# A hybrid decoder layer on one core: weights loaded and split eight blocks at a time instead of four

## The chip, the cores and the metric

The kernel runs on one core of one Trainium2 chip. The metric is the device time of one execution in microseconds (us); the execution is also described by a profile, whose page and trace are quoted here. TensorE (PE) multiplies, VectorE (DVE), ScalarE (ACT) and GpSimd (POOL) do the rest, and SyncE (SP) issues every DMA of this kernel in one queue.

## What is computed

One layer of a decoder on 2048 prompt tokens and 8 one-token samples, 1024 channels wide, all in float32:

```python
h = rmsnorm(x)                                   # norm_pre_mix
q, k, v, z, b, a, mq, mk, mv, mo, mi, mf = split(h @ w_in)          # 3584 columns and 16 gate columns
o_gdn = rmsnorm(gated_delta_rule(conv_silu(q, k, v), ...)) * silu(z)  # 4 heads, chunkwise
h_ml  = sigmoid(mo) * rmsnorm(mlstm(mq, mk, mv, mi, mf))              # 4 heads, chunkwise
x = x + rmsnorm(concat(o_gdn, h_ml) @ w_out)
x = x + rmsnorm(relu(rmsnorm(x) @ w_up) ** 2 @ w_down)               # 4096 hidden channels
```

The outputs are the tokens, the final states of the prompt and the updated states of the samples.

## The kernel before

The prompt is cut into four segments of 512 tokens; the samples ride along with segment 1 (520 columns, worked in two pieces of 260). For each segment the kernel runs the input projection (`a_units`, weights `w_a` and `w_gate`), the two mixers, the output projection (`b_units`, weights `w_o`, worked twice over 256 tokens), and the MLP (`cd_units`, weights `w_up` and `w_dn`). Segments overlap: the mixers and norms of one segment are generators ("streams") that are stepped between the large products of another.

Every large product works on blocks of 128x128 weights. Weights and activations are split into a high and a low float32r part, and a product is three matmuls: high weights by high and by low activations (lines 195 and 196), low weights by high activations (line 200). A **half** (class `Half`) is four weight blocks side by side, a tile of 128x512: `load` brings it into a raw tile `wraw` (four of these, 256 KB), `split` makes its two parts in a tile `whl` (three of these): ACT casts the high part (line 178) and DVE subtracts it from the raw tile for the low part (line 183). `go` issues the 12 matmuls of a half for each piece of columns. A **unit** is two halves; in the projections and the up products both add into one bank of PSUM (`bk`, three banks), in the down products each half has a bank of its own. A raw tile is free for the next load when its split is done, a `whl` tile when the last matmul that reads it is done.

`play` walks the list `main` and sets how far ahead loads and splits are written: at a half it writes the split of the next one and the loads of the four after that, the split with a raised priority (`tc.high_priority(300)`). A scheduler then orders each engine's instructions; every engine, SP's queue included, runs its list in order, so that an instruction that waits holds up what stands behind it. In segment 3 the last states of the samples are worked (`sample_states`): their loads (`st_S`, `st_C`, `dvs`) and stores (`o_sS`, `o_sC`, `o_sn`) share SP's queue with the weights. The products of the last eighth of the MLP run once for each half of the tokens; in segment 3 their split weights are kept for the second half (`keep`, `same`).

Of the kernel before, what the change touches and what calls it, by code (L numbers as in the profile page):

```python
# [24 lines left out]
def program(tc, ctx, d, T):  # L25
# [32 lines left out]
    def r4(t, a=4):  # L58
        return t[:, :].rearrange("p (a b) -> p a b", a=a)

# [25 lines left out]
    w0 = []  # L86
    gain = const([128, 4, 8], "gain")  # channel-major: before and after the mixing, before and after the MLP
    for tt, tag in enumerate(("xt", "xt", "qk", "qk")):
        if tt == 2:
            Q.dma_start(gain, d["gains"])  # L90
            for i in range(2):
                w0.append(sb([128, 512], "wraw", 4))
                Q.dma_start(w0[i], d["w_gate"][:, i * 512:(i + 1) * 512])
        t = sb([128, 1040], tag, 2)
        Q.dma_start(t[:, :1024], d["x_prompt"][tt * 128:(tt + 1) * 128])
        x0.append(t)
        xs0.append(big[:, tt * 1024:(tt + 1) * 1024] if tt < 2 else sb([128, 1040], "xs", 3)[:, :1024])
# [23 lines left out]
    P1 = const([128, 4, 32], "P1")  # L121
# [35 lines left out]
    class Half:  # L157
        """four weight blocks against four activation blocks, each product in three passes; packed weights come twice,
        in columns 32 k + 0..3 and 32 k + 4..7, for the high and the low part of them side by side"""

        def __init__(self, src, acts, parts, first, last, done=None, packed=False):
            self.src, self.acts, self.parts, self.first, self.last, self.done = src, acts, parts, first, last, done
            self.packed = packed
            self.raw = self.hl = self.same = self.keep = None
            self.bank = bk

        def load(self):
            if self.same is not None or self.raw is not None:
                return
            self.raw = sb([128, 512], "wraw", 4)  # L170
            Q.dma_start(self.raw, self.src)

        def split(self):
            if self.same is not None:
                self.hl = self.same.hl
                return
            self.hl = sb([128, 2, 512], "whl", 3, F32R) if self.keep is None else self.keep()
            A.copy(self.hl[:, 0], self.raw)  # L178
            raw, hi, lo = self.raw[:, :], self.hl[:, 0], self.hl[:, 1]
            if self.packed:  # L180
                raw, hi = (t.rearrange("p (a b) -> p a b", b=32)[:, :, 4:8] for t in (raw, hi))
                lo = hi
            V.tensor_tensor(lo, raw, hi.bitcast(F32), op=ALU.subtract)  # L183

        def go(self, part=None):
            acts = self.acts()
            sel = range(len(self.parts)) if part is None else [part]
            for i in sel:
# [4 lines left out]
                for k in range(4):  # L193
                    w = self.hl[:, 0, k * 128:(k + 1) * 128]
# [3 lines left out]
                for k in range(0 if self.packed else 4):  # L198
                    w = self.hl[:, 1, k * 128:(k + 1) * 128]
# [7 lines left out]
    def unit(src, acts, cols, done, packed=False):  # L207
        """acts: a function for the two halves of the activations"""
        parts = [(None, c0, c1) for c0, c1 in cols]
        return [Half(src[:, i * 512:(i + 1) * 512], lambda i=i: acts()[i], parts, i == 0, i == 1, done, packed)  # L210
                for i in range(2)]
# [14 lines left out]
    def norm_a(xt, n, xs=None):  # L226
        """rows / rms"""
        if xs is None:
            xs = sb([128, 1040], "xs", 3)[:, :1024]
# [6 lines left out]
    def norm_b(rows, n, col, gain, halves, bank):  # L236
        """the rows of some token tiles, n tokens in all, to channel-major, times the gain, in two parts"""
# [96 lines left out]
    def a_units(s, halves, order=range(28)):  # L334
# [25 lines left out]
        if s == 0:  # L360
            # the first three of them by token halves, while the second half is being normalised
# [6 lines left out]
    def log1p_exp(L, ab, shape_n):  # L368
        """L = log1p(exp(-ab)), ab >= 0."""
# [1204 lines left out]
```

## Time and profile before

| what | value |
|---|---|
| median of three runs | 2701.5 us (2699.88 to 2704.51) |
| profiled execution, span from first to last instruction | 2703.2 us |
| busy time of PE, DVE, ACT, POOL | 2605.9, 1730.3, 1284.0, 412.8 us |
| mean granted clock of TensorE | 0.989 |
| DMA traffic | 377.41 MB, mean 140 GB/s |

The profiled execution has no time of its own beside its span; the span lies 1.7 us above the median, inside the range of the runs. A busy share is that of the whole span and says nothing about a single stage. In a timeline row the figures are start and duration in us, and the bracket tells how long the engine had been idle before the instruction and what ended that.

### The profile page before, as it was taken

What the parts mean: (1) busy time and instruction counts of PE and PEld (TensorE: products, weight loads), DVE (VectorE), ACT (ScalarE), POOL (GpSimd) and SP (SyncE); (2) the same over time, 40 slices, a digit from 0 to 9 for tenths busy, and PEclk for the clock granted to TensorE, in tenths of its full rate; (3) what the DMA queues carried; (4) which work ended last, traced back from release to release, by engine and by line L of the source; (5) the groups of instructions that cost most, each with busy time, mean ns of one, the idle gap of its engine ahead of it and who ended that gap; (6) DMA issues with size and microseconds to landing.
All of it is one profiled execution on the core that took longest, in us unless ns stands there. A gap on an engine that the chain in (4) does not pass through costs nothing.

```text
span 2703.2 us, 44345 instructions
## 1 busy us (share of the span) xinstructions
PE 2605.9 (96%) x15907; PEld 2271.5 (84%) x15907; DVE 1730.3 (64%) x3508; ACT 1284.0 (48%) x3119; POOL 412.8 (15%) x470
## 2 busy tenths in 40 slices
PE   8999999999999999999799999999999999978998
PEld 6889999778888788878699999997787888766887
DVE  6765768647757557765575865587667567754445
ACT  5636457435535345644455354465363455422332
POOL 2101012311000002420000000062000004430002
PEclk9999999999999999999899999999999999999999
DMA  4444457553323245744433243454242346664222
GB/s 167 156 150 141 145 165 224 193 160 133 102 92 122 99 152 171 238 165 141 97 99 117 95 152 111 153 180 144 88 129 98 123 146 205 205 149 105 94 96 84
DMA packets 319261, 377.41 MB, mean 140 GB/s; under 512 B 53289, under 2 KB 177129, under 8 KB 319033
## 3 DMA queue, kind: packets, MB, share of 16 engines
q1 hardware_dynamic: 319040, 374.57, 44.0%
q8 instruction: 126, 2.06, 0.3%
q14 instruction: 95, 0.77, 0.1%
HBM read 314.04 MB, written 60.53 MB: 139 GB/s over the span
## 4 chain that ended last, share of the span: by engine, by line
PE 83%; DMA 6%; DVE 5%; issue 2%; ACT 2%; POOL 1%; SPq 1%; DVEq 0%; ACTq 0%; POOLq 0%
PE bk L195 25%; PE bk L196 25%; PE bk L200 24%; DVE whl L183 2%; DMA wraw<-w_o 1%; DMA xt<-x_prompt 1%; DVE nt L1197 1%; DMA wraw<-w_up 1%; DVE X L1201 1%; PE mx L563 1%; ACT whl L178 1%; DMA xt<-dO 1%; DMA dqkv<-tB 1%; PE mx L655 1%; PE mx L770 1%
## 5 line engine op out<-in xcount | busy, mean ns | idle before, releaser
L178 ACT CAST whl<-wraw 128x512 fp32r<-128x512 f32 x872 | 539.2, 620 | 972.6 <-PE bk L200 828.6
L183 DVE TENSOR_TENSOR whl<-wraw,whl 128x512 fp32r<-128x512 f32 (+1 forms) x872 | 646.5, 744 | 490.3 <-ACT whl L178 476.1
L195 PE MATMUL bk<-Y,whl 128*128 128x512 f32 (+2 forms) x2208 | 733.2, 346 | 5.7 <-ACT whl L178 3.8
L196 PE MATMUL bk<-Y,whl 128*128 128x512 f32 (+2 forms) x2208 | 731.4, 345 | 0.0
L195 PE MATMUL bk<-X,whl 128*128 128x512 f32 (+3 forms) x2024 | 659.1, 342 | 46.4 <-ACT whl L178 31.8
L196 PE MATMUL bk<-X,whl 128*128 128x512 f32 (+3 forms) x2024 | 656.6, 341 | 2.7 <-DVE X L1201 2.5
L200 PE MATMUL bk<-Y,whl 128*128 128x512 f32 (+2 forms) x2176 | 488.3, 344 | 8.8 <-DVE whl L183 8.8
L195 PEld LDWEIGHTS bk<-Y,whl 128*128 128x128 f32 x2208 | 415.8, 188 | 60.8 <-ACT whl L178 5.9
L195 PEld LDWEIGHTS bk<-X,whl 128*128 128x128 f32 x2024 | 384.1, 190 | 91.7 <-ACT whl L178 35.3
L196 PEld LDWEIGHTS bk<-Y,whl 128*128 128x128 f32 x2208 | 416.7, 189 | 50.3
L200 PE MATMUL bk<-X,whl 128*128 128x512 f32 (+3 forms) x2024 | 442.5, 339 | 8.3 <-DVE whl L183 8.2
L196 PEld LDWEIGHTS bk<-X,whl 128*128 128x128 f32 x2024 | 384.3, 190 | 47.6 <-DVE X L1201 4.1
L200 PEld LDWEIGHTS bk<-Y,whl 128*128 128x128 f32 x2176 | 358.9, 189 | 62.1 <-DVE whl L183 11.5
L200 PEld LDWEIGHTS bk<-X,whl 128*128 128x128 f32 x2024 | 326.6, 189 | 54.1 <-DVE whl L183 11.4
L1245 DVE TENSOR_TENSOR acc<-acc,bk 128x512 f32<-128x512 f32 (+2 forms) x296 | 164.1, 556 | 151.8 <-PE bk L200 147.7
L1124 POOL TENSOR_TENSOR NQ<-NQ,nt 128x256 f32<-128x256 f32 (+4 forms) x145 | 142.8, 988 | 499.0 <-ACT nt L1123 492.1
L1234 DVE TENSOR_TENSOR tB<-tB 128x512 f32<-128x512 f32 (+1 forms) x160 | 93.8, 588 | 55.7 <-ACT Y L1233 54.7
L305 DVE SCALAR_TENSOR_TENSOR tB<-tA,cw,tB 128x512 f32<-128x512 f32 x144 | 107.9, 750 | 13.7 <-ACT tB L301 11.0
L1235 DVE TENSOR_TENSOR Y<-tB,Y 128x512 fp32r<-128x512 f32 (+1 forms) x160 | 97.6, 612 | 3.2
L1232 ACT ACTIVATE tB<-bk 128x512 f32<-128x512 f32 (+1 forms) x160 | 81.7, 511 | 29.2 <-DMA dqkv<-tB 13.1
L1233 ACT ACTIVATE Y<-tB 128x512 fp32r<-128x512 f32 (+1 forms) x160 | 87.3, 549 | 4.3
L596 DVE TENSOR_TENSOR W<-xt 32x30 f32<-32x30 f32 (+14 forms) x240 | 76.2, 317 | 20.0 <-DMA xt<-dn 15.2
(380 smaller groups left out, 2456.4 us busy)
## 6 DMA issues: line engine op xcount, KB each, us to landing
wraw<-w_dn SPq DMA_DIRECT2D x264, 256.0 KB, 2.6
wraw<-w_up SPq DMA_DIRECT2D x256, 256.0 KB, 2.6
wraw<-w_a SPq DMA_DIRECT2D x224, 256.0 KB, 2.8
wraw<-w_o SPq DMA_DIRECT2D x128, 256.0 KB, 3.5
dqkv<-tB SPq DMA_DIRECT2D x48, 256.0 KB, 2.8
gb<-drb SPq DMA_DIRECT2D x32, 256.0 KB, 3.9
qk<-dqkv SPq DMA_DIRECT2D x16, 512.0 KB, 3.7
dzo<-tB SPq DMA_DIRECT2D x32, 256.0 KB, 3.2
```

What stands on the lines that cost most here:

```text
L178: A.copy(self.hl[:, 0], self.raw)
L183: V.tensor_tensor(lo, raw, hi.bitcast(F32), op=ALU.subtract)
L195: PE.matmul(o, lhsT=w, rhs=acts[:, k, 0, c0:c1], start=(self.first and k == 0), stop=False)
L196: PE.matmul(o, lhsT=w, rhs=acts[:, k, 1, c0:c1], start=False, stop=(self.packed and self.last and k == 3))
L200: PE.matmul(o, lhsT=w, rhs=acts[:, k, 0, c0:c1], start=False, stop=(self.last and k == 3))
L305: V.scalar_tensor_tensor(acc, pre[:, t:t + SEG], cw[:, j, t:t + 1], acc, op0=ALU.mult, op1=ALU.add)
L1124: G.tensor_tensor(total[:, c0:c1], total[:, c0:c1], sq[:, c0:c1], op=ALU.add)
L1232: A.activation(r[:, :n], p[:, :n], AF.Relu)
L1233: A.activation(sl[:, 0, c0:c1], r[:, :n], AF.Square)
L1234: V.tensor_tensor(r[:, :n], r[:, :n], r[:, :n], op=ALU.mult)
L1235: V.tensor_tensor(sl[:, 1, c0:c1], r[:, :n], sl[:, 0, c0:c1].bitcast(F32), op=ALU.subtract)
L1245: V.tensor_tensor(a, a, p[:, :c1 - c0], op=ALU.add)
```

## The change

A new class `Weights` holds eight blocks: one raw tile of 128x1024 (two of these instead of four of 128x512), one DMA of 512 KB instead of two of 256 KB, one tile `whl` for both parts (two of 128x2x1024 instead of three of 128x2x512), one cast and one subtraction of 128x1024 instead of two of 128x512. A `Half` now names a `Weights` object and a side of it; in the down products two neighbouring output blocks share one. `play` counts in `Weights`: it writes the split of the next one at the second side of the present one, and keeps two loads written ahead of the last split. The gate weights at the start come in one DMA. In segment 3 the kept weights of the last eighth are two tiles for each `Weights`, so these are still cast and subtracted in pieces of 128x512. To make room, the constant `elast` becomes a broadcast column of `ident`, the scratch tile `P1` of the 32x32 inverses becomes a part of `P2`, and some tiles shrink from 1040 to 1024 columns.

```diff
-    elast = const([128, 128], "elast")
-    G.affine_select(elast, ones, pattern=[[0, 128]], compare_op=ALU.is_ge, fill=0.0, base=-127,
-                    channel_multiplier=1)
-
-    pairsum = const([128, 16], "pairsum")  # high and low part of each gate, added
+    elast = ident[:, 127:128].broadcast_to([128, 128])
...
+    w0 = sb([128, 1024], "wraw", 2)
...
-            for i in range(2):
-                w0.append(sb([128, 512], "wraw", 4))
-                Q.dma_start(w0[i], d["w_gate"][:, i * 512:(i + 1) * 512])
+            Q.dma_start(w0, d["w_gate"])
...
-    P1 = const([128, 4, 32], "P1")
...
+    class Weights:
+        def __init__(self, src, packed=False):
+            self.src, self.packed = src, packed
+            self.raw = self.hl = self.keep = None
+            self.done = False
+        def load(self):
+            if self.raw is None:
+                self.raw = sb([128, 1024], "wraw", 2)
+                Q.dma_start(self.raw, self.src)
+        def split(self):
+            self.hl = sb([128, 2, 1024], "whl", 2, F32R) if self.keep is None else self.keep()
+            for hi, lo, raw in self.pieces():
+                A.copy(hi, raw)
+            for hi, lo, raw in self.pieces():
+                raw, hi = raw, hi
+                if self.packed:
+                    raw, hi = (t.rearrange("p (a b) -> p a b", b=32)[:, :, 4:8] for t in (raw, hi))
+                    lo = hi
+                V.tensor_tensor(lo, raw, hi.bitcast(F32), op=ALU.subtract)
+        def pieces(self):
+            if isinstance(self.hl, list):
+                return [(t[:, 0], t[:, 1], self.raw[:, i * 512:(i + 1) * 512]) for i, t in enumerate(self.hl)]
+            return [(self.hl[:, 0], self.hl[:, 1], self.raw[:, :])]
+        def half(self, i):
+            if isinstance(self.hl, list):
+                return self.hl[i][:, 0], self.hl[i][:, 1]
+            return (self.hl[:, k, i * 512:(i + 1) * 512] for k in range(2))
...
+        def __init__(self, w, side, acts, parts, first, last, done=None):
+            self.w, self.side, self.acts, self.parts = w, side, acts, parts
+            self.first, self.last, self.done, self.packed = first, last, done, w.packed
             self.bank = bk
-
-        def load(self):
-            if self.same is not None or self.raw is not None:
-                return
-            self.raw = sb([128, 512], "wraw", 4)
-            Q.dma_start(self.raw, self.src)
-
-        def split(self):
-            if self.same is not None:
-                self.hl = self.same.hl
-                return
-            self.hl = sb([128, 2, 512], "whl", 3, F32R) if self.keep is None else self.keep()
-            A.copy(self.hl[:, 0], self.raw)
-            raw, hi, lo = self.raw[:, :], self.hl[:, 0], self.hl[:, 1]
-            if self.packed:
-                raw, hi = (t.rearrange("p (a b) -> p a b", b=32)[:, :, 4:8] for t in (raw, hi))
-                lo = hi
-            V.tensor_tensor(lo, raw, hi.bitcast(F32), op=ALU.subtract)
 
         def go(self, part=None):
             acts = self.acts()
+            whi, wlo = self.w.half(self.side)
...
-                    w = self.hl[:, 0, k * 128:(k + 1) * 128]
+                    w = whi[:, k * 128:(k + 1) * 128]
...
-                    w = self.hl[:, 1, k * 128:(k + 1) * 128]
+                    w = wlo[:, k * 128:(k + 1) * 128]
...
+        w = Weights(src, packed)
+        return [Half(w, i, lambda i=i: acts()[i], parts, i == 0, i == 1, done) for i in range(2)]
...
-                A.copy(P1[r:r + 32], pv[r:r + 32])
+                A.copy(P2[r:r + 32, :, 0:32], pv[r:r + 32])
...
-            src = d["w_dn"][e, j // 2][:, (j % 2) * 512:(j % 2 + 1) * 512]
-            return [Half(src, lambda: uT[e], [(None, c0, c1) for c0, c1 in cols], True, True, evac)]
+            if j % 2 == 0:
+                pair[:] = [Weights(d["w_dn"][e, j // 2])]
+            return [Half(pair[0], j % 2, lambda: uT[e], [(None, c0, c1) for c0, c1 in cols], True, True, evac)]
...
-        halves = []
+        ws = []
         for it in main:
             h = it[0] if isinstance(it, tuple) else it
-            if isinstance(h, Half) and h not in halves[-4:]:
-                halves.append(h)
-        place = {id(h): i for i, h in enumerate(halves)}
+            if isinstance(h, Half) and not any(h.w is w for w in ws[-3:]) and not h.w.done:
+                h.w.done = True
+                ws.append(h.w)
+        place = {id(w): i for i, w in enumerate(ws)}
         loaded = split = 0
         for it in main:
             h, part = it if isinstance(it, tuple) else (it, None)
             if not isinstance(h, Half):
                 it()
                 continue
-            n = place[id(h)]
-            while split < min(n + 2, len(halves)):
-                while loaded < min(split + 4, len(halves)):
-                    halves[loaded].load()
+            n = place[id(h.w)]
+            while split < min(n + 2, len(ws)) and (split <= n or h.side == 1 or ws[split].keep is not None):
+                while loaded < min(split + 2, len(ws)):
+                    ws[loaded].load()
                     loaded += 1
                 with tc.high_priority(300):
-                    halves[split].split()
+                    ws[split].split()
                 split += 1
-            while loaded < min(split + 4, len(halves)):
-                halves[loaded].load()
+            while loaded < min(split + 2, len(ws)):
+                ws[loaded].load()
...
+        return [kept[-1][:, i, :, :512] for i in (j % 4, j % 4 + 1)]
...
-        h0.keep, h1.same = lambda j=j: place(j), h0
+        if j % 2 == 0:
+            h0.w.keep = lambda j=j: place(j)
+        h1.w = h0.w
```

The lists of three engines show what moves. First ScalarE at the entry to the output projection of segment 2; line 1084 casts the last tile of its input, line 1093 copies a finished bank, lines 1120 and 1123 square it. Before:

```order
L178 CAST whl<-wraw 128x512
L1084 CAST X_18782<-xt 128x2x256
L178 CAST whl<-wraw 128x512 x7
L1093 COPY Y_19079<-bk 128x256
L1120 ACTIVATE NQ<-bk 128x256
L178 CAST whl<-wraw 128x512 x2
L1093 COPY Y_19079<-bk 128x256
L1123 ACTIVATE nt<-bk 128x256
```

The same place with the change, where the weights' cast is line 169 and the others are 1096, 1105, 1132 and 1135:

```order
L169 CAST whl<-wraw 128x1024
L1096 CAST X_17415<-xt 128x2x256 x2
L169 CAST whl<-wraw 128x1024 x3
L1105 COPY Y_17692<-bk 128x256
L1132 ACTIVATE NQ<-bk 128x256
L169 CAST whl<-wraw 128x1024
L1105 COPY Y_17692<-bk 128x256
L1135 ACTIVATE nt<-bk 128x256
```

For each unit one cast stands where two stood, ahead of the same two readers of the bank; at the entry three of them, for six halves, stand where seven halves stood.

Second SyncE's queue in segment 3, from the stores of the second pair of sample states (`o_sC`, `o_sn`) on. Before:

```order
L171 DMA wraw<-w_up 128x512 x3
L1039 DMA o_sC<-xt 64x8x128
L1040 DMA o_sn<-xt 64x8x1
L171 DMA wraw<-w_up 128x512
L1039 DMA o_sC<-xt 64x8x128
L1040 DMA o_sn<-xt 64x8x1
L171 DMA wraw<-w_up 128x512
L171 DMA wraw<-w_dn 128x512 x8
```

With the change:

```order
L164 DMA wraw<-w_up 128x1024 x2
L1051 DMA o_sC<-xt 64x8x128
L1052 DMA o_sn<-xt 64x8x1
L1051 DMA o_sC<-xt 64x8x128
L1052 DMA o_sn<-xt 64x8x1
L164 DMA wraw<-w_up 128x1024
L164 DMA wraw<-w_dn 128x1024 x4
```

Before, one half of `w_up` is issued between the two pairs of stores and one behind them; with the change one load of 128x1024 stands behind both pairs. Up to the first of these stores both lists issue the same number of weight blocks.

Third ScalarE at the start, around the square of the first tile of segment 1 (line 231, then 243) for which a load of `x_prompt` must land. Before:

```order
L178 CAST whl<-wraw 128x512
L231 ACTIVATE xs,st<-xt 128x1024
L178 CAST whl<-wraw 128x512 x2
L338 ACTIVATE grow<-mx,gbias 128x256
L300 COPY tA<-bk 128x256
L301 ACTIVATE tB<-bk,cw 128x256
L178 CAST whl<-wraw 128x512
```

With the change:

```order
L350 ACTIVATE grow<-mx,gbias 128x256
L243 ACTIVATE xs,st<-xt 128x1024
L312 COPY tA<-bk 128x256
L313 ACTIVATE tB<-bk,cw 128x256
L169 CAST whl<-wraw 128x1024
L350 ACTIVATE grow<-mx,gbias 128x256
L169 CAST whl<-wraw 128x1024
```

The square still stands ahead of the cast of the second unit's weights; two readers of a bank (lines 312 and 313) now stand between them, and the cast is one of 128x1024.

## Rows read from the trace of the kernel before

**Rows 1.** The page: span, then busy time, share and instructions of each engine.

```profile
span 2703.2 us, 44345 instructions
PE 2605.9 (96%) x15907; PEld 2271.5 (84%) x15907; DVE 1730.3 (64%) x3508; ACT 1284.0 (48%) x3119; POOL 412.8 (15%) x470
```

**Rows 2.** The page: groups, busy us, mean ns, then idle before and releasers.

```profile
L178 ACT CAST whl<-wraw 128x512 fp32r<-128x512 f32 x872 | 539.2, 620 | 972.6 <-PE bk L200 828.6
L183 DVE TENSOR_TENSOR whl<-wraw,whl 128x512 fp32r<-128x512 f32 (+1 forms) x872 | 646.5, 744 | 490.3 <-ACT whl L178 476.1
```

**Rows 3.** Waits of TensorE: total us, times, longest us.

```profile
PE bk L195 <- ACT whl L178: 35.6, 17, 9.8
PE bk L200 <- DVE whl L183: 17.0, 17, 2.7
PE bk L195 <- ACT tB L1232: 16.2, 3, 12.6
```

**Rows 4.** Timeline, ScalarE, an up product: start us, us, what [idle <-releaser].

```profile
703.65 0.62 ACT L178 CAST whl<-wraw 128x512 fp32r<-128x512 f32 x1 [1.01 <-PE bk L200]
706.45 0.62 ACT L178 CAST whl<-wraw 128x512 fp32r<-128x512 f32 x1 [2.17 <-PE bk L200]
```

**Rows 5.** Timeline, ScalarE, output projection of segment 2.

```profile
1743.52 0.62 ACT L178 CAST whl<-wraw 128x512 fp32r<-128x512 f32 x1 [0.79 <-PE bk L200]
...
1744.92 0.62 ACT L178 CAST whl<-wraw 128x512 fp32r<-128x512 f32 x1 [0.23 <-PE bk L200]
...
1746.33 0.62 ACT L178 CAST whl<-wraw 128x512 fp32r<-128x512 f32 x1 [0.78 <-PE bk L200]
```

**Rows 6.** Timeline, VectorE, the same stretch.

```profile
1744.17 0.69 DVE L183 TENSOR_TENSOR whl<-wraw,whl 128x512 fp32r<-128x512 f32 x1 [0.71 <-ACT whl L178]
```

**Rows 7.** Groups by line with shapes kept apart: the splits of 128x1024.

```profile
L552 DVE TENSOR_TENSOR xs<-qk,xs 128x1024 fp32r<-128x1024 f32 x16 | 19.5, 1222 | 13.5 <-PE mx L563 6.5 <-ACT xs L551 6.1 <-PE mx L244 0.8
...
L551 ACT CAST xs<-qk 128x1024 fp32r<-128x1024 f32 x16 | 16.8, 1052 | 20.8 <-DMA qk<-dqkv 20.8
```

**Rows 8.** DMA issues of the whole span: KB each, median us to landing.

```profile
wraw<-w_up SPq DMA_DIRECT2D x256, 256.0 KB, 2.6
...
xt<-x_prompt SPq DMA_DIRECT2D x14, 512.0 KB, 3.6
```

**Rows 9.** DMA issues of 1742 to 1764 us, output projection of segment 2.

```profile
wraw<-w_o SPq DMA_DIRECT2D x16, 256.0 KB, 3.0
```

**Rows 10.** DMA issues of 424 to 472 us, output projection of segment 0.

```profile
wraw<-w_o SPq DMA_DIRECT2D x22, 256.0 KB, 5.0
```

**Rows 11.** Windows: stretch, length, busy us of PE, PEld, DVE, ACT, POOL, PEclk, DMA.

```profile
424.00:472.00 48.00, 45.92 (x393) 45.12 (x392) 40.44 (x116) 37.01 (x100) 14.23 (x17) 1.00 0.75 232
...
1742.00:1764.00 22.00, 22.00 (x190) 22.00 (x189) 10.73 (x17) 14.01 (x31) 5.20 (x7) 1.00 0.56 191
...
2370.00:2460.00 90.00, 64.35 (x258) 49.24 (x257) 39.31 (x41) 19.57 (x34) 27.14 (x16) 0.91 0.71 141
```

**Rows 12.** Timeline, SyncE, sample states of segment 3.

```profile
2415.02 0.63 SPq L1039 DMA_DIRECT2D o_sC<-xt  x1
...
2444.44 0.63 SPq L1039 DMA_DIRECT2D o_sC<-xt  x1
...
2446.13 0.65 SPq L171 DMA_DIRECT2D wraw<-w_up  x1
...
2448.21 1.14 SPq L171 DMA_DIRECT2D wraw<-w_up  x1
```

**Rows 13.** Timeline, ScalarE, the same stretch.

```profile
2456.94 0.62 ACT L178 CAST whl<-wraw 128x512 fp32r<-128x512 f32 x1 [13.61 <-DMA wraw<-w_up]
...
2459.28 1.17 ACT L178 CAST whl<-wraw 128x512 fp32r<-128x512 f32 x2 [0.56 <-DMA wraw<-w_up]
```

**Rows 14.** Timeline, ScalarE, the start.

```profile
28.51 1.06 ACT L231 ACTIVATE xs<-xt 128x1024 f32<-128x1024 f32 x1 [4.63 <-DMA xt<-x_prompt]
```

**Rows 15.** Timeline, VectorE, end of the output projection of segment 2.

```profile
1775.67 1.23 DVE L183 TENSOR_TENSOR whl<-wraw,whl 128x512 fp32r<-128x512 f32 x1
```

More of the change, by code (lines that the diff above doesn't have):

```diff
@@ L90, in program @@
             Q.dma_start(gain, d["gains"])
-            for i in range(2):
-                w0.append(sb([128, 512], "wraw", 4))
-                Q.dma_start(w0[i], d["w_gate"][:, i * 512:(i + 1) * 512])
-        t = sb([128, 1040], tag, 2)
+            Q.dma_start(w0, d["w_gate"])
+        t = sb([128, 1040 if tag == "xt" else 1024], tag, 2)
         Q.dma_start(t[:, :1024], d["x_prompt"][tt * 128:(tt + 1) * 128])
         x0.append(t)
-        xs0.append(big[:, tt * 1024:(tt + 1) * 1024] if tt < 2 else sb([128, 1040], "xs", 3)[:, :1024])
+        xs0.append(big[:, tt * 1024:(tt + 1) * 1024] if tt < 2 else sb([128, 1024], "xs", 3)[:, :1024])
     cw = const([128, 12, 4], "cw")
@@ L157, in program @@
     class Half:
[L161 to L164, printed above, removed]
+        def __init__(self, w, side, acts, parts, first, last, done=None):
+            self.w, self.side, self.acts, self.parts = w, side, acts, parts
+            self.first, self.last, self.done, self.packed = first, last, done, w.packed
@@ L209, in unit @@
         parts = [(None, c0, c1) for c0, c1 in cols]
-        return [Half(src[:, i * 512:(i + 1) * 512], lambda i=i: acts()[i], parts, i == 0, i == 1, done, packed)
-                for i in range(2)]
+        w = Weights(src, packed)
+        return [Half(w, i, lambda i=i: acts()[i], parts, i == 0, i == 1, done) for i in range(2)]
     def prompt_part(p, c0, c1):
@@ L228, in norm_a @@
         if xs is None:
-            xs = sb([128, 1040], "xs", 3)[:, :1024]
+            xs = sb([128, 1024], "xs", 3)[:, :1024]
         st = sb([128, 4], "st", 4)
@@ L514, in gdn_half @@
             n = hf * 2 + i
-            t = sb([128, 1040], "qk", 2)[:, :1024].rearrange("p (a b) -> p a b", a=8)
+            t = sb([128, 1024], "qk", 2)[:, :1024].rearrange("p (a b) -> p a b", a=8)
             Q.dma_start(t, dqkv[s][0:8, :, n * 128:(n + 1) * 128].rearrange("j p t -> p j t"))
@@ L549, in gdn_half @@
             t = qkv[i]
-            hi, lo = (sb([128, 1040], "xs", 3, F32R)[:, :1024].rearrange("p (a b) -> p a b", a=8) for _ in range(2))
+            hi, lo = (sb([128, 1024], "xs", 3, F32R)[:, :1024].rearrange("p (a b) -> p a b", a=8) for _ in range(2))
             A.copy(hi, t)
@@ L626, in gdn_half @@
                 for r in (0, 64):
-                    PE.matmul(p[r:r + 32, h * 32:(h + 1) * 32], lhsT=P1[r + 32:r + 64, h],
+                    PE.matmul(p[r:r + 32, h * 32:(h + 1) * 32], lhsT=P2[r + 32:r + 64, h, 0:32],
                               rhs=Yd[r + 32:r + 64, i * 4 + h, r + 32:r + 64], start=True, stop=True)
@@ L788, in sample_mix @@
         for j0, j1 in ((0, 8), (8, 12)):
-            cb = sb([128, 1040], "qk", 2)[:, :1024].rearrange("p (a b) -> p a b", a=8)
+            cb = sb([128, 1024], "qk", 2)[:, :1024].rearrange("p (a b) -> p a b", a=8)
             Q.dma_start(cb[:24, :j1 - j0], d["st_conv"][:, :, j0 * 128:j1 * 128].rearrange("b r (j c) -> (b r) j c", c=128))
@@ L1163, in load @@
         def load(j):
-            t = sb([128, 1040], tag, 3 if tag == "xs" else 2)[:, :k * w].rearrange("p (a b) -> p a b", a=k)
+            t = sb([128, 1040 if tag == "xt" else 1024], tag, 3 if tag == "xs" else 2)[:, :k * w].rearrange("p (a b) -> p a b", a=k)
             Q.dma_start(t, src[j:j + k, :, c0:c1].rearrange("j p t -> p j t"))
@@ L1220, in cd_units @@
     def cd_units(s, h2, sums):
-        uT = {}
+        uT, pair = {}, []
         def up(f):
@@ L1236, in up, with down @@
             return unit(d["w_up"][f], lambda: h2, pieces(s), evac)
-        def down(e, j, cols):
+        def down(e, j, cols, pair):
             def evac(parts):
@@ L1262, in cd_units @@
             for j in range(8):
-                us += down(e, j, pieces(s))
+                us += down(e, j, pieces(s), pair)
         whole = 1 <= s < NSEG - 1
@@ L1268, in cd_units @@
             for j in range(8):
-                tail[-1] += down(7, j, cols)
+                tail[-1] += down(7, j, cols, pair)
         return us[:ups], us[ups:], tail
@@ L1391, in program @@
     a0 = a_units(0, hX)
-    for (h, _), w in zip(a0, w0):
-        h.raw = w
+    a0[0][0].w.raw = w0
     main += a0[:30]
```

2 lines of the change are left out of this document (removed).

## The prediction

> **What bounds the kernel now.** I read the page's busy times first: TensorE is busy 2605.9 of 2703.2 us [rows 1], so all its idle time together is 97 us, and a gain can only come out of that. Then the groups of the split [rows 2]: 872 casts of a mean 620 ns and 872 subtractions of a mean 744 ns; before a cast ScalarE is idle most often because TensorE has still to free the `whl` tile (828.6 of 972.6 us): the split is early and waits for TensorE. Then the waits of TensorE [rows 3]: 35.6 us for ScalarE's cast (17 times), 17.0 us for VectorE's subtraction (17 times), 16.2 us for a `tB` in front of the products. So about 53 us of the span is late weights, in some thirty places.
>
> The timeline of an up product [rows 4] shows the ordinary stage: a cast follows the last matmul of the half that held its tile, 2.80 us after the one before. With three `whl` tiles a cast that starts when half k-3 ends is needed when k-1 ends, 5.60 us later, and takes 0.62. In the output projection a half has 256 columns: a unit of two casts lasts 1746.33-1743.52 = 2.81 us, 1.40 a half [rows 5], and the subtraction takes 0.69 [rows 6]. Each segment has 16 such units, in two passes of eight.
>
> **The change, part by part.**
>
> *(a) Fewer, larger instructions.* The split of 128x1024 that the kernel already has elsewhere takes 1.222 us on VectorE and 1.052 on ScalarE [rows 7]. Two casts of 0.62 become one of 1.05, 0.19 less; two subtractions of 0.69 become one of 1.22, 0.16 less. Over 436 units that is 82 us of ScalarE and 70 of VectorE, but TensorE's matmuls stay as they are. In an ordinary stage I cost it at nothing: the split of a unit now takes 1.05+1.22 = 2.27 us and can start when the unit before the present one ends, 5.60 us ahead of its first use; the 3.3 us left over is the cover, and while it lasts neither a gain nor a loss shows.
>
> The Trainium skill, page "VectorE: DVE Perf Modes", section on the TRN2 errata, says that each instruction has a fixed cost, so that one large tile pays it once where small ones pay it each time. The rows agree (1.22 against 1.38). By that rule alone the change would be faster wherever VectorE is waited for; that is the second rival below, priced there from rows.
>
> *(b) The raw tiles in the output projection.* A raw tile goes round in landing + cast + subtraction. Before, four of them: (3.0+0.62+0.69)/4 = 1.08 us a half with the landing of that stretch [rows 9], against the 1.40 that TensorE takes, so no load is late. Now there are two tiles of eight blocks. The landing of 512 KB is not seen for weights; the nearest row is `x_prompt`, 3.6 against 2.6 of a 256 KB load of `w_up` [rows 8]. In this projection 256 KB took 3.0, and 3.6 x 3.0/2.6 = 4.2; I take 4.0. The tile then goes round in (4.0+1.05+1.22)/2 = 3.14 us a unit against 2.81, so each unit comes 0.33 us later once the lead is spent. The lead: a subtraction is over 2.27 us after its release, and is needed after 2.81 + 0.94 (low parts are the last third of a half, 8/12 x 1.40) = 3.75, so 1.5 us, four units. In segment 2 TensorE is at its full pace there (busy 22.00 of 22.00 us [rows 11]) and the passes follow each other: (16-4) x 0.33 = 4 us. In segment 0 it is crowded: 22 half loads in 48 us [rows 10, 11], 4.36 us a unit; with 6.0 to land the tile goes round in 4.13, just inside. In segments 0, 1 and 3 other work fills part of the time; I choose a third of 4 us for each, 4 in all. Term: +8. Bounds: 0 if the load lands in 3.3 us or less (2 x 2.81 - 2.27); 4 x 16 x 0.33 = 21 if all projections ran at that pace.
>
> The Trainium skill, page "SBUF — State Buffer", section "The DMA setup-cost knee", speaks for large transfers: about 2 us fixed and the rest by bytes, worked out (an estimate) 2.6 us for 256 KB and 3.2 for 512 KB. The first agrees with the 2.6 of the row, the second stands below its 3.6. With 3.2 in place of 4.0 the loop would be 2.74 and the term 0; I go by the row.
>
> *(c) Crowded ends of the projections.* Beside GpSimd a subtraction of 128x512 took 1.23 us instead of 0.69 [rows 15]. One of 128x1024 there is bounded by 1.22 and 2.46. It must be whole before the low parts of even the first half: some +1 us a place, against 0.16 saved on each of about eight units. Eight places, net 0, bounds -6 and +6.
>
> *(d) The sample states.* SP's queue runs in order. Before, one half of `w_up` is issued between two pairs of stores, at 2446.13, and one behind them, at 2448.21 [rows 12]; ScalarE stood 13.61 us for the first and cast it at 2456.94, the second at 2459.28 [rows 13]; TensorE was busy 64.35 of the 90 us around it [rows 11]. With the change the one load stands behind both pairs, so its cast can't start ahead of about 2459.28: 2.34 later and 0.43 longer, +3. Both sides: 0 if the 512 KB overtake the 10.8 us that 256 KB needed there, 8 if the pairs of stores ahead of these (from 2415.02 on) cost as much again.
>
> *(e) The start.* ScalarE's square of an `x_prompt` tile waits 4.63 us and ends at 29.57 [rows 14]; the split behind it is now 0.43 longer and two readers of a bank have come ahead of it: +1, bounds -1 and 3.
>
> *(f) At no cost.* `elast` and `P1` touch small float32 products and copies whose counts stay; gain or loss under 1 us. The wait for `tB` [rows 3] hangs on stores of a convolution state, ahead of which the queue holds as many weight blocks as before: unchanged.
>
> Sum: 8 + 0 + 3 + 1 = +12 us on the span of 2703.2, which lies 1.7 above the median; on the median **2713.5 us**.
>
> **Rivals.**
> 1. *No change.* The 512 KB land within 3.3 us, (b) is 0 and (d), (e) stay under 4 us: 2702 to 2706. For it: DMA engines are 0.56 busy in that projection [rows 11], and `x_prompt` landed in 3.6 beside other loads. Against: 3.6 is already above 3.3.
> 2. *Faster.* The waits for VectorE (17.0 us, 17 times [rows 3]) fall on places where splits are queued behind other work of an engine that is short of time; each unit now asks for 0.16 and 0.19 us less, and a second half never waits, since its parts are made with the first. If half of these waits go and (b) is 0, 2701.5 - 8.5 = 2693. It decides if the subtraction beside GpSimd stays under some 1.8 us and the landing under 3.3. Against: the whole tile must now be done before the first half starts.
> 3. *Crowding all over.* Landings of 6 us as in segment 0 (where 256 KB took 5.0 [rows 10]) in every projection: (6.0+2.27)/2 = 4.13 against 2.81 where TensorE is undisturbed, 16 x 1.3 = 21 us in one segment alone: 2724 to 2735.
>
> **How the numbers follow.** Forecast, slower by 6 to 23 us: 0.48. Rival 3: 0.10. No change: 0.22. Faster: 0.20. This kernel's measurement can tell about 0.2%, 5.4 us: faster is below 2696.1, slower above 2706.9. The chances are 0.20, 0.22 and 0.58. The range that leaves out no more than two in ten reaches from 2693, the faster rival's own time, to 2728, inside the third's; the forecast's own range is 2707 to 2724.
>
> **What the trace will show.** (a) right: some 430 casts near 1.05 us and subtractions near 1.22, ScalarE and VectorE busy some 80 and 70 us less, and in up products casts still released by TensorE. (b) right: the landing of `w_o` near 4 us, ScalarE in the output projection idle for a DMA of `wraw`, TensorE no longer 22 of 22 us there; wrong if casts there still wait for TensorE. (c) subtractions beside GpSimd under or over 1.8 us, and the waits of TensorE for VectorE below or above 17.0 us. (d) ScalarE's wait of 13.61 us some 2.3 us longer, and TensorE busy less than 64 of 90 us there. What would make the whole wrong is a quick landing of 512 KB, which removes two thirds of the sum, or waits of the second halves that were a larger part of the 53 us than I took.

## The result and the profile after

The changed kernel takes 2719.72 us (median of 4 runs, 2716.67 to 2725.43) where the kernel before took 2701.58: a ratio of **1.0065, interval 1.0047 to 1.0083**, 18 us slower. The forecast was 2713.5, its own range 2707 to 2724. The profiled executions stand 13.6 us apart (2716.8 and 2703.2). The stages below are read from these two, so 4.5 of the 18 us have no place in what follows.

The page of the changed kernel, busy times and the two groups of the split, as [rows 1] and [rows 2]:

```profile
span 2716.8 us, 41794 instructions
PE 2617.1 (96%) x15907; PEld 2277.5 (84%) x15907; DVE 1662.8 (61%) x3072; ACT 1215.2 (45%) x2683; POOL 447.4 (16%) x469
...
L175 DVE TENSOR_TENSOR whl<-wraw,whl 128x1024 fp32r<-128x1024 f32 (+1 forms) x436 | 551.3, 1265 | 503.1 <-ACT whl L169 501.1
L169 ACT CAST whl<-wraw 128x1024 fp32r<-128x1024 f32 x436 | 456.7, 1048 | 845.6 <-PE bk L212 660.9
```

Its waits of TensorE, as [rows 3] (total, times, longest):

```profile
PE bk L207 <- ACT whl L169: 34.5, 17, 6.9
PE bk L207 <- ACT tB L1244: 18.3, 2, 15.8
PE bk L212 <- DVE whl L175: 16.5, 17, 3.8
```

ScalarE and VectorE are relieved of 69 and 67 us, and TensorE waits for them as long as before. All its idle time grew by 2.4 us, from 97.3 to 99.7; the other 11.2 stand in its busy time, which is longer at a lower clock and hides short waits. So where the time went has to be read by place. The same copies out of a bank are found in both traces by their order on their line; the start of each with the change, less its start before, is how far the change is behind at that point (times of the kernel before):

| up to | behind, us | what lies between |
|---|---|---|
| 200 us | -0.5 | the start |
| 540 us | +10.7 | output projection and norms of segment 0 |
| 1200 us | +12.7 | the MLP of segment 0, output projection of segment 1 |
| 1700 us | +11.8 | the MLP of segment 1, mixers |
| 1900 us | +17.1 | output projection of segment 2 |
| 2340 us | +18.5 | the MLP of segment 2, output projection of segment 3 |
| 2480 us | +13.6 | the sample states |
| the end | +13.6 | |

**Segment 2.** ScalarE and VectorE in the first pass of its output projection (start, us; idle before and who ended it):

```profile
1751.94 1.05 ACT L169 CAST whl<-wraw 128x1024 fp32r<-128x1024 f32 x1 [1.77 <-PE bk L212]
1754.85 1.05 ACT L169 CAST whl<-wraw 128x1024 fp32r<-128x1024 f32 x1 [1.30 <-DMA wraw<-w_o]
1758.63 1.05 ACT L169 CAST whl<-wraw 128x1024 fp32r<-128x1024 f32 x1 [2.18 <-DMA wraw<-w_o]
1761.51 1.05 ACT L169 CAST whl<-wraw 128x1024 fp32r<-128x1024 f32 x1 [1.27 <-DMA wraw<-w_o]
1764.34 1.05 ACT L169 CAST whl<-wraw 128x1024 fp32r<-128x1024 f32 x1 [1.22 <-DMA wraw<-w_o]
```

```profile
1753.02 1.23 DVE L175 TENSOR_TENSOR whl<-wraw,whl 128x1024 fp32r<-128x1024 f32 x1 [1.59 <-ACT whl L169]
1755.93 1.22 DVE L175 TENSOR_TENSOR whl<-wraw,whl 128x1024 fp32r<-128x1024 f32 x1 [1.69 <-ACT whl L169]
```

Up to 1751.94 the cast still waits for TensorE, then for the load: (1764.34-1754.85)/3 = 3.16 us a unit in the mean, but one step of 3.78 beside two of 2.88 and 2.83. A subtraction frees a raw tile, at 1753.02+1.23 = 1754.25 and 1757.15, and the load that follows is cast at 1758.63 and 1761.51: 4.4 us from the free tile to the landed one, and 3.4 for the two around them, 3.9 in the mean. So a few late loads carry the delay.

TensorE doesn't feel it at once. From the first matmul of a unit to that of the next it takes 2.81 us, as before, until 1763, and no more than 2.87 until 1771.54. Only then is the lead spent; the next unit starts 3.81 us later:

```profile
1775.36 0.39 PE L207 MATMUL bk<-X,whl 128*128 128x256 f32 x1 [0.69 <-ACT whl L169]
```

From the first unit to the last of both passes it takes 48.6 us (1748.92 to 1797.52) where before it took 45.8: 2.8 us lost, 1.1 of them up to here. The norms behind the passes make it 5.3.

**Segment 0.** SP's queue, then VectorE, ScalarE and TensorE, in the output projection and where the next input projection starts:

```profile
434.80 0.33 SPq L164 DMA_DIRECT2D wraw<-w_o  x1
...
443.33 0.88 SPq L1094 DMA_DIRECT2D xt<-dO  x2
...
473.34 0.38 SPq L1177 DMA_DIRECT2D xt<-xT  x1
474.43 19.35 SPq L164 DMA_DIRECT2D wraw<-w_a  x4
```

```profile
473.19 1.21 DVE L175 TENSOR_TENSOR whl<-wraw,whl 128x1024 fp32r<-128x1024 f32 x1
...
514.11 2.29 DVE L175 TENSOR_TENSOR whl<-wraw,whl 128x1024 fp32r<-128x1024 f32 x1
```

```profile
483.97 1.04 ACT L169 CAST whl<-wraw 128x1024 fp32r<-128x1024 f32 x1 [4.80 <-DMA wraw<-w_a]
...
507.67 1.03 ACT L169 CAST whl<-wraw 128x1024 fp32r<-128x1024 f32 x1
```

```profile
447.60 0.39 PE L207 MATMUL bk<-X,whl 128*128 128x256 f32 x1 [1.97 <-ACT X L1096]
...
485.06 0.79 PE L207 MATMUL bk<-Y,whl 128*128 128x512 f32 x1 [3.52 <-ACT whl L169]
...
516.45 2.07 PE L212 MATMUL bk<-Y,whl 128*128 128x512 f32 x4 [3.77 <-DVE whl L175]
```

and TensorE at the last of these places in the kernel before:

```profile
505.13 2.07 PE L200 MATMUL bk<-Y,whl 128*128 128x512 f32 x4 [2.46 <-DVE whl L183]
...
510.80 1.20 PE L200 MATMUL bk<-Y,whl 128*128 128x512 f32 x4 [1.22 <-DVE whl L183]
```

There are three stalls. The first, 1.97 us, is not for weights but for the projection's own input `X`: the load of the mixer's output (`dO`) is issued at 443.33, before the change at 431.85. Loads of `w_o` that wait for a raw tile stand ahead of it in SP's queue (the one of 434.80 for a tile freed at 434.77); whether they are what makes it late was not tried. Second, a raw tile is free at 474.40, its load of `w_a` is issued at 474.43 behind a 512 KB load of `xT`, and the cast can start only at 483.97, 9.5 us later; TensorE stands 3.52 us. Third, the cast of another unit is over at 508.70, but VectorE, whose list holds the norm's instructions ahead, comes to the subtraction at 514.11 and takes 2.29 us for it (beside GpSimd): 3.77 us. The third is no loss of the change: the kernel before stands 2.46 and 1.22 us there for its own late subtractions, and the change is as far behind ahead of this place as past it (10.3 us by the matmuls of line 207 at 490 and at 540). Then the clock (windows of the changed kernel; PEclk is the third figure from the end):

```profile
450.00:460.00 10.00, 10.00 (x74) 9.59 (x73) 8.16 (x24) 7.62 (x18) 3.51 (x3) 0.83 0.53 179
...
480.00:490.00 10.00, 6.48 (x23) 4.91 (x22) 1.62 (x2) 1.97 (x4) 1.15 (x1) 0.83 0.50 177
...
510.00:520.00 10.00, 6.23 (x20) 4.64 (x19) 10.00 (x8) 6.43 (x11) 9.25 (x6) 0.76 0.94 287
520.00:530.00 10.00, 10.00 (x44) 8.20 (x43) 5.59 (x6) 2.90 (x4) 4.71 (x3) 0.89 0.55 174
```

and windows of the kernel before:

```profile
480.00:490.00 10.00, 10.00 (x48) 8.25 (x48) 4.73 (x8) 3.21 (x7) 2.08 (x2) 1.00 0.31 109
500.00:510.00 10.00, 7.08 (x23) 4.71 (x21) 10.00 (x8) 4.24 (x7) 7.55 (x5) 0.83 0.74 254
```

At the end of each stall or just behind it TensorE ran at 1.2 instead of 2.4 GHz: for 3.4 us at the first (450.43 to 453.84), 3.4 at the second (484.56 to 487.97) and 6.8 at the third (515.28 to 522.11); before, for 3.4 at the stall of 2.46. It was busy for 3.4, 2.9 and 5.7 us of these, and half of that is lost: 1.7, 1.5 and 2.8 us. So of the 11 us lost between 200 and 490 about 3 are the clock's, 5 longer stalls (8.6 us against 3.8, stalls over 0.1 us), and the rest, some 3, is in no stall that can be seen.

**The sample states**, SP, ScalarE and TensorE, as [rows 12, 13]:

```profile
2454.06 0.63 SPq L1051 DMA_DIRECT2D o_sC<-xt  x1
...
2457.66 0.93 SPq L164 DMA_DIRECT2D wraw<-w_up  x1
```

```profile
2469.87 1.04 ACT L169 CAST whl<-wraw 128x1024 fp32r<-128x1024 f32 x1 [14.54 <-DMA wraw<-w_up]
```

```profile
2470.97 0.79 PE L207 MATMUL bk<-X,whl 128*128 128x512 f32 x1 [6.71 <-ACT whl L169]
```

The one load does stand behind both pairs of stores, and its cast comes 15.8 us after the first store instead of 12.5, 3.3 later, as forecast. But TensorE's stall is 6.71 us where before it was 8.19:

```profile
2457.61 0.79 PE L195 MATMUL bk<-X,whl 128*128 128x512 f32 x1 [8.19 <-ACT whl L178]
```

It had weights left until 10.2 us after that store, before only until 5.0; and the earlier stalls there shrank too (from 9.75 to 6.90 us the largest). TensorE was busy 71 of the 90 us from 2380 to 2470, where before it was 64 of 90 [rows 11].

### The profile page after: what moved, and what is told of

Read it like the earlier page. It is cut to its first block, busy times and chain, and to the rows that moved or that the text cites. A ratio compares the mean times of both kernels' runs of the same rounds, so it can differ in the third digit from the quotient of the medians.

```text
span 2716.8 us, 41794 instructions
## 1 busy us (share of the span) xinstructions
PE 2617.1 (96%) x15907; PEld 2277.5 (84%) x15907; DVE 1662.8 (61%) x3072; ACT 1215.2 (45%) x2683; POOL 447.4 (16%) x469
## 4 chain that ended last, share of the span: by engine, by line
PE 79%; DMA 8%; DVE 6%; ACT 3%; POOL 2%; issue 1%; SPq 1%; DVEq 0%; ACTq 0%; POOLq 0%
PE bk L207 23%; PE bk L208 23%; PE bk L212 23%; DMA wraw<-w_o 2%; DVE whl L175 2%; ACT whl L169 1%; DVE nt L1209 1%; DMA dqkv<-tB 1%; PE mx L575 1%; POOL NQ L1136 1%; DVE X L1213 1%; DVE nt L1318 1%; PE mx L667 1%; DMA wraw<-w_dn 1%; PE mx L693 1%
## 5 line engine op out<-in xcount | busy, mean ns | idle before, releaser
L175 DVE TENSOR_TENSOR whl<-wraw,whl 128x1024 fp32r<-128x1024 f32 (+1 forms) x436 | 551.3, 1265 | 503.1 <-ACT whl L169 501.1
L169 ACT CAST whl<-wraw 128x1024 fp32r<-128x1024 f32 x436 | 456.7, 1048 | 845.6 <-PE bk L212 660.9
L207 PE MATMUL bk<-Y,whl 128*128 128x512 f32 (+2 forms) x2208 | 733.2, 347 | 10.7 <-ACT whl L169 7.3
L212 PEld LDWEIGHTS bk<-Y,whl 128*128 128x128 f32 x2176 | 359.3, 189 | 61.7 <-DVE whl L175 11.2
L212 PEld LDWEIGHTS bk<-X,whl 128*128 128x128 f32 x2024 | 329.0, 190 | 56.1 <-DVE whl L175 13.6
L1136 POOL TENSOR_TENSOR NQ<-NQ,nt 128x256 f32<-128x256 f32 (+4 forms) x145 | 157.5, 1088 | 473.9 <-ACT nt L1135 449.8
```

The costliest lines, as they stand in the source:

```text
L169: A.copy(hi, raw)
L207: PE.matmul(o, lhsT=w, rhs=acts[:, k, 0, c0:c1], start=(self.first and k == 0), stop=False)
L212: PE.matmul(o, lhsT=w, rhs=acts[:, k, 0, c0:c1], start=False, stop=(self.last and k == 3))
L1136: G.tensor_tensor(total[:, c0:c1], total[:, c0:c1], sq[:, c0:c1], op=ALU.add)
```

## The experiments

Two theories. **A**: a raw tile is held from the issue of its load to the end of its split, and two of them are too few where TensorE needs a unit every 2.81 us. **B**: the long instructions themselves, the subtraction above all, which the first low part waits for and which stand in front of other work. The runs e, f and g were made on three chips, and on each the kernel before took 2707 to 2708 us; a ratio is to the kernel before on the same chip, with its 95% interval. The change itself was run apart from these, where the kernel before took 2701.6.

| run | raw tiles | loads | whl tiles | cast, subtraction | ratio (interval) |
|---|---|---|---|---|---|
| the change | 2 x 1024 | 512 KB | 2 x 1024 | 1024, 1024 | 1.0065 (1.0047 to 1.0083) |
| e1 | 2 x 1024 | 512 KB | 4 x 512 | 512, 512 | 0.9977 (0.9964 to 0.9989) |
| e2 | 2 x 1024 | 256 KB | 2 x 1024 | 1024, 1024 | 1.0076 (1.0055 to 1.0098) |
| e3 | 4 x 512 | 256 KB | 4 x 512 | 512, 512 | 0.9959 (0.9946 to 0.9972) |
| e4 | 3 x 1024 | 512 KB | 2 x 1024 | 1024, 1024 | 0.9950 (0.9934 to 0.9966) |
| f1 | 2 x 1024 | 512 KB | 2 x 1024 | 512, 512 | 0.9991 (0.9981 to 1.0000) |
| f2 | 4 x 512 | 256 KB | 3 x 512 | 512, 512 | 1.0001 (0.9991 to 1.0011) |
| f3 | as before | as before | as before | as before | 0.9999 (0.9990 to 1.0008) |
| f5 | 2 x 1024 | 512 KB | 2 x 1024 | 1024, 1024 | 1.0043 (1.0028 to 1.0058) |
| g1 | 2 x 1024 | 512 KB | 2 x 1024 | 1024, 512 | 1.0067 (1.0054 to 1.0079) |
| g2 | 2 x 1024 | 512 KB | 2 x 1024 | 512, 1024 | 1.0067 (1.0055 to 1.0079) |
| g3 | 3 x 1024 | 512 KB | 4 x 512 | 512, 512 | 0.9852 (0.9839 to 0.9865) |
| g4 | 5 x 512 | 256 KB | 4 x 512 | 512, 512 | 0.9922 (0.9909 to 0.9935) |

e4, f5 and g3 have one tile `tA` instead of two; e4, f5, g3 and g4 two tiles `nt` instead of three.

**e1.**

```diff
-            self.hl = sb([128, 2, 1024], "whl", 2, F32R) if self.keep is None else self.keep()
+            self.hl = [sb([128, 2, 512], "whl", 4, F32R) for _ in range(2)] if self.keep is None else self.keep()
```

> The changed kernel with its load of 512 KB into two raw tiles of 128x1024, but each unit cast and subtracted in two pieces of 128x512, in two tiles whl of their own (four of 128x2x512, the same memory as before this edit). Theory A, the raw tiles (landing, cast and subtraction of a whole unit go round in two tiles): the tile is free after about 2.0 us of splitting instead of 2.27, the loop is (4.0 + 2.0)/2 = 3.0 us a unit against 2.81, so most of the 18 us stays: 2712 to 2718. Theory B, the size of the split (the low part of the first half waits for a subtraction of the whole unit, which on a busy VectorE comes late): the loss goes, 2700 to 2706, and the waits of TensorE for VectorE fall back to some 17 us.

0.23% below the kernel before: outside A's figure, below B's. B is ahead, or A's sum was wrongly worked; e4 speaks against B.

**e2.**

```diff
...
-                Q.dma_start(self.raw, self.src)
+                for i in range(2):
+                    Q.dma_start(self.raw[:, i * 512:(i + 1) * 512], self.src[:, i * 512:(i + 1) * 512])
```

> The changed kernel with two DMAs of 256 KB into each raw tile of 128x1024; cast and subtraction still of 128x1024. Theory A: the cast needs both, the raw tile is freed as late as in the change: 2714 to 2722, no gain. Theory B: the same, 2716 to 2722. If the large transfer itself were the cause (a slower landing of 512 KB than of two halves), 2700 to 2708.

As the change: the intervals overlap. The size of the transfer is not the cause.

**e3** combines e1's edit with a DMA of 256 KB into each of four raw tiles:

```diff
...
-                self.raw = sb([128, 1024], "wraw", 2)
-                Q.dma_start(self.raw, self.src)
+                self.raw = [sb([128, 512], "wraw", 4) for _ in range(2)]
+                for i in range(2):
+                    Q.dma_start(self.raw[i], self.src[:, i * 512:(i + 1) * 512])
```

> The code of the changed kernel, with its order of writing loads and splits by whole units, its merged constants and smaller tiles, but four raw tiles of 128x512 with a DMA each and four whl tiles of 128x2x512. Theories A and B: back at the kernel before, 2698 to 2706. A third theory, that the order in units (loads written later, SP's queue another) or the merged constants cost the time: 2712 or more.

0.41% below the kernel before, a gain that neither theory has; f2 and f3 look for it.

**e4.**

```diff
...
-                self.raw = sb([128, 1024], "wraw", 2)
+                self.raw = sb([128, 1024], "wraw", 3)
...
-        pre = sb([128, 3 + SEG], "tA", 2)
+        pre = sb([128, 3 + SEG], "tA", 1)
...
-        return sb([128, SEG + NB], "nt", 3)
+        return sb([128, SEG + NB], "nt", 2)
```

> The changed kernel with three raw tiles of 128x1024 instead of two; the room comes from one tile tA instead of two and two tiles nt instead of three. Theory A: the loop of the raw tiles is (4.0 + 2.27)/3 = 2.09 us a unit, under 2.81, and the late casts of the output projections go: 2702 to 2710 (the fewer tiles tA and nt may cost a few us). Theory B: unchanged, 2716 to 2724.

0.50% below, with the large split: against B, and more than A has, by which it should come no lower than the kernel before. In segment 2's projection its casts wait for TensorE again, 2.81 us apart:

```profile
1757.85 1.05 ACT L169 CAST whl<-wraw 128x1024 fp32r<-128x1024 f32 x1 [1.21 <-PE bk L212]
1760.66 1.05 ACT L169 CAST whl<-wraw 128x1024 fp32r<-128x1024 f32 x1 [1.21 <-PE bk L212]
```

In segment 0 the wait of 3.5 us for a late load is gone, but TensorE still waits for `X`, and longer:

```profile
456.09 0.58 PE L207 MATMUL bk<-X,whl 128*128 128x256 f32 x1 [4.50 <-ACT X L1096]
```

**f1** keeps one whl tile for a unit and cuts only the instructions:

```diff
-            return [(self.hl[:, 0], self.hl[:, 1], self.raw[:, :])]
+            cs = [slice(i * 512, (i + 1) * 512) for i in range(2)]
+            return [(self.hl[:, 0, c], self.hl[:, 1, c], self.raw[:, c]) for c in cs]
```

> The changed kernel with the unit cast and subtracted in two pieces of 128x512, but inside its one whl tile of 128x2x1024 (two of these), so that the first piece can't start before the whole unit two places back is done. In the run with pieces in tiles of their own the first half could start half a unit earlier. Theory A1 (the raw tile is held too long because the split starts only when a whole whl tile is free): only the 0.3 us of pipelining between the engines is gained, 0.3 to 0.7% above the kernel before, like the change. Theory B1 (the size of the pieces itself: the wait of the first low part and the blocking of ScalarE and VectorE by long instructions): within 0.3% of the kernel before, as the run with pieces in tiles of their own.

The figure of B1: the pieces alone bring back 0.74%, all that the change lost; tiles of their own add 0.14 (e1). A1, the late start of the split, falls. Its casts in segment 2:

```profile
1754.53 1.14 ACT L169 CAST whl<-wraw 128x512 fp32r<-128x512 f32 x2 [0.96 <-DMA wraw<-w_o]
1757.45 1.14 ACT L169 CAST whl<-wraw 128x512 fp32r<-128x512 f32 x2 [1.22 <-DMA wraw<-w_o]
1760.40 1.14 ACT L169 CAST whl<-wraw 128x512 fp32r<-128x512 f32 x2 [1.26 <-DMA wraw<-w_o]
1762.72 1.14 ACT L169 CAST whl<-wraw 128x512 fp32r<-128x512 f32 x2 [0.62 <-DMA wraw<-w_o]
```

Two casts take 1.14 us and the second subtraction ends 0.8 later: the tile is free after 1.94 us, not 2.27. The units are 2.73 us apart, (1762.72-1754.53)/3, just under the 2.81 that TensorE needs: the same loop as in A, on the good side of the threshold. That takes the landings of this run, 3.5 us in the mean here; with the change's 3.9 the loop would be 2.92.

**f2**, e3 with `"whl", 3`:

> The run with small loads and small splits (11 us faster than the kernel before) with three whl tiles of 128x2x512 instead of four, so that its buffers are those of the kernel before and only the order in units, the merged constants and the smaller tiles differ. If the fourth whl tile made the 11 us: within 0.2% of the kernel before. If the order in units or the merges made them: again 0.3 to 0.5% below.

No change from the kernel before: the order in units costs nothing, and e3's 0.41% is the fourth whl tile's. With three and with four tiles TensorE waits:

```profile
PE bk L209 <- ACT whl L171: 31.9, 14, 10.4
PE bk L214 <- DVE whl L177: 19.8, 19, 3.7
```

```profile
PE bk L209 <- ACT whl L171: 22.4, 7, 8.8
PE bk L214 <- DVE whl L177: 9.7, 10, 1.9
```

**f3**, the kernel before with the merged constants and smaller tiles alone:

> The kernel before with only the merges of the change: elast as a broadcast column of ident, P1 inside P2, tiles of 1024 instead of 1040 columns. The prediction costs them at under 1 us: within 0.2% of the kernel before. If they made the 11 us of the run with small loads and splits: 0.3 to 0.5% below.

No change, as the prediction had it.

**f5**, e4's edits to `tA` and `nt` with two raw tiles:

> The control of the run with three raw tiles: the changed kernel with one tile tA instead of two and two tiles nt instead of three, but its two raw tiles. If the third raw tile made that run 32 us faster than the change: 0.6 to 1.0% above the kernel before, as the change or somewhat slower. If the fewer tiles tA and nt did it (by another order of the work): 0.3% or more below the kernel before.

0.43% above the kernel before, short of the range but on the side of the third raw tile: against this control it is worth 0.93%. The fewer tiles `tA` and `nt` cost nothing that these runs show.

**g1, g2**: f1's pieces for the subtraction alone, and for the cast alone. The argument of `pieces` says whether to cut; g1's edit, with `True` and `False` the other way round in g2:

```diff
-            for hi, lo, raw in self.pieces():
+            for hi, lo, raw in self.pieces(False):
                 A.copy(hi, raw)
-            for hi, lo, raw in self.pieces():
+            for hi, lo, raw in self.pieces(True):
...
```

> The changed kernel (two raw tiles of 128x1024, two whl tiles of 128x2x1024) with one cast of 128x1024 and two subtractions of 128x512. Theory A (a raw tile is held from its landing to the end of its split; two of them go round in (landing + split)/2): the split lasts 1.05 + 0.69 + 0.69 = 2.43 us, with the landing of 3.9 us seen in segment 2 that is 3.17 us a unit against 2.81, as in the change: 0.4 to 0.8% above the kernel before. Theory B (the long subtraction, which the first low part waits for and which stands before VectorE's other work): within 0.2% of the kernel before.

> The counterpart: two casts of 128x512 and one subtraction of 128x1024. Theory A: the split lasts 1.13 + 1.22 = 2.35 us, the loop 3.13 us a unit: 0.4 to 0.8% above the kernel before. Theory B with the subtraction at fault: the same 0.5 to 0.8% above. If the long cast is at fault (the high part comes 0.43 us later, ScalarE's other work waits): within 0.2% of the kernel before.

Both as the change, as A has it, and against B: cutting the long subtraction alone doesn't help, nor the long cast alone. What the two share with the change is a split of over 2.2 us on two raw tiles. A's loop of 3.17 us for g1 is too high, though: its landings were 3.3 to 3.5 us in that pass and the units some 2.9 apart, so g1 lost little there and most in segment 0 (11.8 us behind at 540). That its total came out as A had it is in part luck.

**g3**, e1 with three raw tiles, and **g4**, e3 with five:

> Three raw tiles of 128x1024, one DMA of 512 KB each, but split in pieces of 128x512 into four whl tiles of 128x2x512; room from one tile tA and two tiles nt, as in the run with three raw tiles. Theory A: with three raw tiles the split's length no longer matters, so no more than the run with three raw tiles and the large split: 0.4 to 0.6% below the kernel before. Theory B: the small split adds its own gain, 0.8% or more below.

> The run with small loads and small splits (0.41% below the kernel before) with five raw tiles of 128x512 instead of four; room from two tiles nt instead of three. Theory A: four tiles of 128x512 already go round in (3.0 + 0.62 + 0.69)/4 = 1.08 us a half against 1.40, so a fifth adds little: 0.3 to 0.6% below the kernel before. If late loads in the crowded stretches (landings of 5 us and more) still cost: 0.7% or more below.

Both are faster than A allows: g3 1.48% below the kernel before (2667 us), the fastest of all, and g4 0.78%, the figure given for late loads in crowded stretches. The largest waits of TensorE in g3, and the one for the subtraction:

```profile
PE bk L207 <- ACT whl L169: 12.3, 4, 5.0
PE mx L256 <- DVE NQ L245: 8.5, 2, 8.0
PE bk L207 <- DVE acc L1257: 7.5, 1, 7.5
PE bk L207 <- ACT tB L1244: 4.6, 1, 4.6
...
PE bk L212 <- DVE whl L175: 0.3, 1, 0.3
```

Of the 53 us that TensorE waited for late weights before, 12.6 are left, and the wait for `tB` has gone from 16 us to 4.6.

**By place.** What each run's profiled execution loses on the kernel before (us; a minus is a gain), reckoned as in the table of the result. f3 is in effect the same kernel as before, so what it shows, up to 3 us, is how far one execution can differ from another.

| run | segment 0, 200 to 540 | 540 to 1700 | segment 2, 1700 to 1900 | 1900 to 2340 | sample states |
|---|---|---|---|---|---|
| f3 | 1.1 | -1.1 | -0.1 | 0.3 | 2.6 |
| the change | 11.2 | 1.1 | 5.3 | 1.4 | -4.9 |
| e2, f5, g1, g2 (long cast or subtraction) | 9.2 to 12.9 | 2.2 to 3.7 | 3.0 to 9.8 | 2.2 to 3.9 | -6.1 to -3.8 |
| f1 (both cut) | 0.8 | -2.8 | -0.3 | 3.0 | -2.9 |
| e1 (both cut, four whl tiles) | 4.0 | -1.5 | -1.4 | 1.9 | -4.8 |
| e4 (three raw tiles) | 5.4 | -7.1 | -0.2 | -1.4 | -12.6 |
| g3 (three raw tiles, both cut) | -5.2 | -13.8 | -3.7 | 0.4 | -12.6 |
| f2 (4 x 512 raw) | 2.0 | -2.2 | 0.8 | 1.9 | 0.5 |
| e3 (4 x 512 raw, four whl tiles) | 0.9 | -5.6 | 0.7 | -3.7 | 0.3 |
| g4 (5 x 512 raw, four whl tiles) | -3.8 | -5.9 | -1.1 | 0.3 | -5.5 |

In segment 2 it is as A has it: a loss with two raw tiles and a long split, none with three or with a short split. In segment 0, where most was lost, the third raw tile takes away some 4 us of its control's 9.2, and cutting both instructions takes away more; A doesn't explain that. And of the 30 us by which e4 beats f5 in these stages, 10.6 lie between 540 and 1700 and 8.7 in the sample states, where the change had lost little or won: so that a third raw tile makes the kernel fast again doesn't show that it undoes the same loss.

## Why the prediction was right, and where not

- **(a)** held: the casts take 82 us less, the subtractions 95 (the mean of the small ones had been 0.74, not 0.69), though VectorE is relieved of 67 only, since its other work took 28 more. In ordinary stages nothing came of it; most of the casts' wait is still for TensorE (660.9 of 845.6 us).
- **(b)** In segment 2 the mechanism is shown. The loop was put at 3.14 us a unit with a landing of 4.0, and the casts went at 3.16 with 3.9; the two passes lost 2.8 us where 4 were forecast (the norms behind made it 5.3). A third raw tile takes the loss away, a split 0.3 us shorter too. Two things there came out otherwise. The delay was not 0.33 in each unit but one late load here and there, and the sign "TensorE no longer 22 of 22 us there" did not show: from 1749 to 1771 it was busy 22.00 of 22.00 us, as the lead lasted nearly the whole first pass. **The step that failed is the sum for segment 0**, "with 6.0 to land the tile goes round in 4.13, just inside", and so a third of 4 us: 11 us were lost. A mean landing under the threshold says little in a crowded stretch: one load of 9.5 us made a stall of 3.52, and a late `X` one of 1.97. The clock behind the stalls, which the prediction didn't price, added 3 us to them. That the raw tiles made all of this is not shown, since with three of them 5 us are still lost there. The stretches with projections together lost some 20 us, not 8; that this is near the upper bound of 21 is chance, for the bound is of a loop that runs in all projections.
- **(c)** The waits for VectorE stayed at 17 us, net 0 as forecast; a contended subtraction took 2.29 us, near the upper bound.
- **(d)** failed in its sign: -5 instead of +3. The cast is late by what was worked out; what was not asked is how far TensorE's stock of split weights then reaches. The raw tiles set it: the change and all six runs with two raw tiles for whole units won 3 to 6 us in this stretch, the two with three of them 12.6, and e3 and f2, with four of half a unit, none (g4, with five, 5.5). How they do it is not settled. Loads that wait for a raw tile stand ahead of the states' loads in SP's queue, and with one raw tile for a unit there are half as many such places; that was not tried by itself.
- **(e)** -0.5 us against +1, and **(f)** (f3; the wait for `tB` 15.8 us after the change) were as small as said.
- The rivals: no change would have needed landings of 3.3 us, and 3.4 to 4.4 were measured in segment 2; the waits that the faster rival hoped to halve did not move; crowding all over came in one segment only.
- That the sum of +12 us stands close to the 13.6 between the two traces is luck: (b) was 12 us too low and (d) 8 too high.

What stays open is why the threshold is so sharp over the whole kernel (a split of 1.94 us costs nothing, one of 2.3 us 0.7%; 10 us of the difference lie in segment 0), and what the small pieces with whl tiles of their own add once there are three raw tiles (0.98% from e4 to g3): A says nothing should be left. Piece size and the fourth whl tile were not parted there; the traces put 10.6 us of the gain in segment 0 and 6.7 between 540 and 1700, where the wait for `tB` is.

## What to carry to other kernels

Merging loads and instructions makes a buffer be held longer (here 6.2 us, 3.9 + 2.3, instead of the 4.3 of the prediction's sum), and halves the number of buffers for the same memory: before doing it, work out (landing + all that reads the buffer)/(number of buffers) against the pace of the fastest consumer, with single late landings and not the mean of the stretch. Memory freed for larger instructions may be worth more as another buffer: here a fourth tile of split weights gave 0.41%, and a third raw tile turned 0.43% slower into 0.50% faster. Price a new stall with the clock behind it.

## What the runs showed of the hardware

Stalls of TensorE of 1.97, 3.52 and 3.77 us were followed by 3.4, 3.4 and 6.8 us at the lower of its two clock levels (granted 0.83, 0.83, 0.76 and 0.89 in windows of 10 us), of which it was busy 3.4, 2.9 and 5.7 us; so the clock cost another 40 to 90% of the stall. And a load of 512 KB of weights for which the cast waited took from 3.2 us (1086.60 to 1089.79) to 16.6 (1328.46 to 1345.08) from issue to its cast. In the case of 9.5 us the DMA engines were nearly idle after its issue (9 GB/s from 477 to 479 us), for a reason that no run shows.
